# Gate rows as four products side by side, the last key transpose one tile later, and the branch stage's first operands over a token chunk, in a hybrid diffusion layer

## The chip, the cores and the metric

The kernel runs on one core of a Trainium2 chip. The metric is the device time of one execution in microseconds (us); the median of three runs of the kernel before is 2556.35 us (2554.89 to 2567.19). Engines are called as the profile calls them: PE (TensorE matmul), PEld (its weight load), DVE (VectorE), ACT (ScalarE), POOL (GpSimd) and SP (SyncE, which issues most of the transfers).

## What is computed

One layer of a hybrid backbone on 256 prompt tokens and 2048 latent tokens, width 1024, all in fp32:

```python
shift, scale, gate = split(silu(cond) @ w_mod + b_mod, 3)      # w_mod 1024 x 3072
xm = rmsnorm(x, norm_g) * (1 + scale) + shift
q, k, v, g_na, u, g_lru, c_b, c_c, c_h, g_conv, m_na, m_lru, m_conv = split(xm @ w_in)
o_na   = attention(q, k, v)            # prompt: dense; latents: neighbourhood + cached keys
h_f + h_b = two gated linear recurrences over conv4(u)
o_conv = c_b * conv3(c_c * c_h)
merged = ( sigmoid(m_na)   * ((o_na * silu(g_na))         @ w_br_na)
         + sigmoid(m_lru)  * (((h_f + h_b) * silu(g_lru)) @ w_br_lru)
         + sigmoid(m_conv) * ((o_conv * silu(g_conv))     @ w_br_conv) )
x = x + gate * (merged @ w_out);  y = rmsnorm(x, final_g)
# outputs: y of both groups, k and v of the prompt, final recurrence states
```

`cond` has two rows: one vector for the prompt, one for the latents. So `gate` is two rows of 1024 numbers.

## The kernel before

**Tokens and products.** Tokens stand in five chunks: chunk 0 is the prompt (256 tokens), chunks 1 to 4 are 512 latents each. A large product in fp32 is done as three passes of a split operand (high part and rest): `xh*whi`, `xl*whi`, `xh*wlo`. One 128-column tile of `w_in` times one 512-token chunk is thus 8 x 3 = 24 matmuls on PE into one bank of PSUM (tile `psM_C` is weight tile M with chunk C; `w_in_chunk`, L147 to L155). Only two chunks of latents and the prompt fit at a time, so the projection runs twice: with chunks in `ORDA` = (1, 2, 0), then in `ORDB` = (3, 4). The normalised chunks stand in tiles `xhA`/`xlA` (chunks 1, later 3) and `xhB`/`xlB` (2, later 4).

**Order.** Each engine takes its instructions in the order in which the program emits them. `dense` runs over weight tiles and chunks; a `Side` generator gets one step after each chunk (`tick`), and so lays recurrences, attention units or the gate rows between the chunks. Transfers are issued by SP in program order, a few by ACT. A transfer waits on its queue until the memory it writes is free, and all behind it wait too.

**Gate rows** (`gate_rows`, L382 to L399). The third kilocolumn of `w_mod` times the two condition vectors `sc`: for each half of 512 columns, eight products (one per 128 rows of `w_mod`) of two output rows each, `TE.matmul(pgt[:2, :], sc[:, kk - 1, :], ...)` in plain fp32, one after each chunk of the q and k tiles. The weights come in pieces `wg` of 256 KB, two buffers, one step ahead. Two sums on DVE (L398) add the bias.

**Prompt keys.** When tile 4+j has met the prompt chunk, the keys are copied to `kc` (ACT, L376) and put on a list; `key_out` (L343 to L351) transposes them on PE (`ktr`, two transposes) and stores them. For the last one this is called right after the last key tile (7), before tile 12.

**Branch stage and its memory** (L917 to L950). The last tiles of the projection (58 to 63, merge gates) run with ORDB; meanwhile the branch weights are loaded and split (`load_wb`). Then pool `p1` is closed, and the pool `zp` opens at the place in memory that is free. For chunk c and branches 2, 1, 0 it loads 1024 KB of branch outputs (`zr`, half of that for the prompt), splits them (`zh` on ACT, `zl` on DVE), loads eight `tg` tiles of gates, and does eight times 12 matmuls `pb`. Results are merged on POOL (L944) and stored by ACT (`d_mrg`). `zp` lies in memory over what `p1` held: weight buffers and chunk tiles. A first write into a place waits for the last reader of what lay there.

**Output stage** (L953 to L1000). Pool `op` opens where `zp` lay. `load_m` reads merged rows `mr`, splits them into `mh`, `ml`; PE does 24 matmuls `po` for each 128 tokens and half; the first 128 tokens come from tiles `m0h`, `m0l` that were made earlier. The first load of the stage is `mr128` (L958, called at L963).

Of the kernel before, what the change touches and what calls it, by code (L numbers as in the profile page):

```python
# [7 lines left out]
F32 = mybir.dt.float32  # L8
BF16 = mybir.dt.bfloat16
F32R = mybir.dt.float32r  # L10
AF = mybir.ActivationFunctionType
ALU = mybir.AluOpType
# [3 lines left out]
P = 128  # L16
D = 1024
KD = 8
# [3 lines left out]
ORDA, ORDB = (1, 2, 0), (3, 4)  # L22
# [22 lines left out]
def build(nc, tc, H):  # L45
    es = ExitStack()
    V, S, G, TE, SY = nc.vector, nc.scalar, nc.gpsimd, nc.tensor, nc.sync
# [25 lines left out]
    def scratch(name, shape):  # L73
        return tc.dram_tile(shape, F32, name=name)
# [9 lines left out]
    d_gna = scratch("d_gna", [512, T])  # L84
# [4 lines left out]
    d_sig = scratch("d_sig", [3072, T])  # L89
# [19 lines left out]
    sc = cp.tile([P, 8, 2], F32, tag="sc", name="sc")  # L109
# [9 lines left out]
    def bank(name):  # L119
        return psA.tile([P, 512], F32, tag="bank", name=name, bufs=8)  # L120


    p1 = ExitStack()
    ep = p1.enter_context(tc.tile_pool(name="ep", bufs=2))
    wp = p1.enter_context(tc.tile_pool(name="wp", bufs=2))
    xp = p1.enter_context(tc.tile_pool(name="xp", bufs=1))
    x0s = ExitStack()
    x0p = x0s.enter_context(tc.tile_pool(name="x0p", bufs=1))
    XS = {1: "A", 2: "B", 3: "A", 4: "B", 0: "0"}
# [8 lines left out]
    def load_w(m):  # L138
        hi = wp.tile([P, KD, P], F32R, tag="whi", name=f"whi{m}", bufs=3)
        lo = wp.tile([P, KD, P], F32R, tag="wlo", name=f"wlo{m}", bufs=3)  # L140
        for q in (0, 1):
            raw = wp.tile([P, 4, P], F32, tag="wraw", name=f"wraw{m}_{q}", bufs=4)
            SY.dma_start(raw, H["w_in"][m][:, 4 * q : 4 * q + 4, :])
            split(raw, hi[:, 4 * q : 4 * q + 4, :], lo[:, 4 * q : 4 * q + 4, :], G)
        return hi, lo

    def w_in_chunk(m, w, ci, evac):  # L147
        hi, lo = w
        t0, n = CH[ci]
        ps = bank(f"ps{m}_{ci}")  # L150
        ps_ = passes(KD)
        for i, (k, a, b) in enumerate(ps_):
            TE.matmul(ps[:, :n], (lo if a else hi)[:, k, :], (xl if b else xh)[ci][:, k, :],  # L153
                      start=(i == 0), stop=(i == len(ps_) - 1))
        evac(ci, t0, n, ps[:, :n])  # L155
# [8 lines left out]
    def ev_tanh(dst, j):  # L164
        def f(ci, t0, n, ps):
            o = ep.tile([P, 512], F32, tag="ev", bufs=3, name="evm")
            S.activation(o[:, :n], ps, AF.Tanh, scale=0.5)  # L167
            S.dma_start(dst[j * P : (j + 1) * P, t0 : t0 + n], o[:, :n])
        return f

    def ev_silu(dst, j):

        def f(ci, t0, n, ps):
            t = ep.tile([P, 512], F32, tag="evt", name="evt")
            o = ep.tile([P, 512], F32, tag="ev", bufs=3, name="evs")
            S.activation(t[:, :n], ps, AF.Tanh, scale=0.5)
            V.scalar_tensor_tensor(o[:, :n], t[:, :n], 1.0, ps, ALU.add, ALU.mult)
            SY.dma_start(dst[j * P : (j + 1) * P, t0 : t0 + n], o[:, :n])
        return f
# [17 lines left out]
    def dense(tiles, order, side=None):  # L197
        for m, evac in tiles:
            w = load_w(m)
            for ci in order:  # L200
                w_in_chunk(m, w, ci, evac)
                if side:
                    side.tick()
# [32 lines left out]
    with tc.tile_pool(name="p0", bufs=2) as p0:  # L236
# [13 lines left out]
        for kk in range(KD):  # L250
            wm = wms[kk // 2][:, kk % 2, :]
            SY.dma_start(wm, H["w_mod"][kk * P : (kk + 1) * P, 0 : 2 * D])
            for i in range(4):
                TE.matmul(pm[i][:2, :], sc[:, kk, :], wm[:, i * 512 : (i + 1) * 512],
                          start=(kk == 0), stop=(kk == KD - 1))
# [125 lines left out]

    def gate_rows(eq):  # L382

        for hf in (0, 1):
            hs = slice(512 * hf, 512 * hf + 512)
            bg = ep.tile([P, 512], F32, tag="evt", name=f"bg{hf}")
            SY.dma_start(bg[:2, :], H["b_gate"][:, hs].broadcast_to([2, 512]))
            pgt = bank(f"pgt{hf}")
            nxt = []
            for kk in range(KD + 1):  # L390
                if kk < KD:
                    wg = eq.tile([P, 512], F32, tag="wg", name=f"wg{hf}_{kk}", bufs=2)
                    SY.dma_start(wg, H["w_mod"][kk * P : (kk + 1) * P, 2048 + 512 * hf : 2560 + 512 * hf])
                    nxt.append(wg)
                if kk:
                    TE.matmul(pgt[:2, :], sc[:, kk - 1, :], nxt.pop(0), start=(kk == 1), stop=(kk == KD))
                yield
            V.tensor_tensor(bg[:2, :], pgt[:2, :], bg[:2, :], ALU.add)  # L398
            SY.dma_start(d_gate[:, hs], bg[:2, :])  # L399

    def cached_keys(eq):
# [248 lines left out]
    def flush():  # L650
        while pend or tpd:
            advance()
            yield
# [145 lines left out]
    def chain(*gens):  # L799
        for g in gens:  # L800
            yield from g
# [5 lines left out]
    with tc.tile_pool(name="eq", bufs=2, reuse_waits="tile") as eq, \  # L807
            tc.tile_pool(name="vcA", bufs=2, reuse_waits="tile") as vc, \
            tc.tile_pool(name="lp", bufs=1, reuse_waits="tile") as lp:
        lru = Side(lru_steps(lp, False), 17 / 84)  # L810
        gr = Side(gate_rows(eq), 1)
        dense([(j, ev_hilo(eq, d_q, j, 0.125, False)) for j in range(4)], ORDA,
              Side(iter(lambda: (lru.tick(), gr.tick()), None), 1))
        cached_keys(eq)
        dense([(4 + j, ev_hilo(eq, d_k, j, 1.0, True)) for j in range(4)], ORDA,
              Side(iter(lambda: (lru.tick(), gr.tick()), None), 1))
        gr.drain()
        while deferred:
            key_out(eq, *deferred.pop(0))
        dense([(12 + j, ev_silu(d_gna, j)) for j in range(4)], ORDA, lru)  # L820
        for j in range(4):
            dense(conv_tiles(vc, j, ORDA), ORDA, lru)
        lru.drain()
    with tc.tile_pool(name="atA", bufs=2, reuse_waits="tile") as at:
        AT[0] = at
        first_loads, units = latent_steps(at, [0])
        side = Side(chain(prompt_steps(at, first_loads), units, flush()), 60 / 60)
# [22 lines left out]
    with tc.tile_pool(name="lpB", bufs=1, reuse_waits="tile") as lp:  # L850
        lru = Side(lru_steps(lp, True), 25 / 76)
# [11 lines left out]
    with tc.tile_pool(name="atB", bufs=2, reuse_waits="tile") as at:  # L863
# [6 lines left out]
        side = Side(chain(units, flush()), 101 / 27)  # L870
# [4 lines left out]
    wbs = ExitStack()  # L875
# [13 lines left out]

    wks = (8, 9, 10, 11, 4, 5, 6, 7, 0, 1, 2, 3)  # L890
    for i, m in enumerate(range(18, 24)):
        dense([(40 + m, ev_tanh(d_sig, m))], ORDB)
        for k in wks[2 * i : 2 * i + 2]:
            load_wb(k)
    p1.close()

    wor = es.enter_context(tc.tile_pool(name="wor", bufs=1, reuse_waits="tile"))
    m0h = wor.tile([P, KD, P], F32R, tag="m0h", name="m0h")
    m0l = wor.tile([P, KD, P], F32R, tag="m0l", name="m0l")

# [15 lines left out]
    with tc.tile_pool(name="zp", bufs=2, reuse_waits="tile") as zp:  # L916
        for c in (0, 1, 2, 3, 4):  # L917
            t0, n = CH[c]
            cs = slice(t0, t0 + n)
            acc = []  # L920
            if c == 2:
                load_m0()
            for br in (2, 1, 0):
                zr = zp.tile([P, 4, 512], F32, tag="zraw", name=f"zr{c}_{br}", bufs=1)
                zh = zp.tile([P, 4, 512], F32R, tag="zh", name=f"zh{c}_{br}", bufs=3)
                zl = zp.tile([P, 4, 512], F32R, tag="zl", name=f"zl{c}_{br}", bufs=3)
                SY.dma_start(zr[:, :, :n], d_z[br * 512 : (br + 1) * 512, cs].rearrange("(k p) t -> p k t", p=P))
                for k in range(4):
                    split(zr[:, k, :n], zh[:, k, :n], zl[:, k, :n])
                for m in range(8):  # L930
                    t = zp.tile([P, 512], F32, tag="acc" if br == 2 else "tg", name=f"tg{c}_{br}_{m}",
                                bufs=9 if br == 2 else 6)
                    SY.dma_start(t[:, :n], d_sig[br * D + m * P : br * D + (m + 1) * P, cs])
                    ps = bank(f"pb{c}_{m}_{br}")
                    ps_ = passes(4)
                    for i, (k, a_, b_) in enumerate(ps_):
                        TE.matmul(ps[:, :n], (wbl if a_ else wbh)[br * 4 + k][:, m * P : (m + 1) * P],  # L937
                                  (zl if b_ else zh)[:, k, :n], start=(i == 0), stop=(i == len(ps_) - 1))

                    V.scalar_tensor_tensor(t[:, :n], t[:, :n], 1.0, ps[:, :n], ALU.add, ALU.mult)  # L940
                    if br == 2:
                        acc.append(t)
                    else:
                        G.tensor_tensor(acc[m][:, :n], acc[m][:, :n], t[:, :n], ALU.add)  # L944
                    if br == 0:
                        S.dma_start(d_mrg[m * P : (m + 1) * P, cs], acc[m][:, :n])
                if c == 4 and br:

                    for k in range(4):
                        load_wo(k + 4 * (2 - br), k + 4 * br)  # L950


    with tc.tile_pool(name="op", bufs=2, reuse_waits="tile") as op:  # L953
# [9 lines left out]
        nxt = load_m(P, P)  # L963
# [117 lines left out]
```

## Time and profile before

| | |
|---|---|
| median of three runs | 2556.35 us (2554.89 to 2567.19) |
| profiled execution, own time | 2558.7 us |
| its span (first to last instruction) | 2556.9 us |
| granted TensorE clock, mean | 0.989 |
| PE busy | 2492.1 us (97% of the span) |
| DVE / ACT / POOL busy | 1096.7 / 976.5 / 878.3 us |
| DMA | 360.84 MB, mean 141 GB/s |

PE is busy nearly all the time, so a microsecond is won either where PE has less to do, or in one of the few places where it waits. Busy counts overlap: a pipelined matmul of 512 columns has a duration of some 0.39 us in the list but starts 0.23 us after the one before it, so costs on PE are read from the distance of starts. A granted clock of 1.00 is 2.4 GHz and 0.50 is 1.2 GHz; after some of its waits PE runs a few us at the lower level.

### The profile page before, as it was taken

Reading aid. Unit: us, or ns where it says so; the run is one execution under the profiler, and the core shown is the slowest. Engines: PE = TensorE matmul, PEld = TensorE weight load, DVE = VectorE, ACT = ScalarE, POOL = GpSimd, SP = SyncE. Lnnn points to the kernel's source line nnn. Section 1 sums busy time; section 2 is a strip of 40 time slices with the busy share of each in tenths; the row PEclk is TensorE's granted clock in tenths of the full one; section 3 lists DMA queues with packets and bytes.
Section 4 is the critical chain, followed back from the end, with each engine's and each line's share of the span. In section 5 each row is a group of like instructions: output and inputs, shape, how many; then the busy total and the mean of one; then the engine's idle time right before and its main releaser. Section 6 shows DMA issues by size and latency. Waiting matters only on the chain. (4 is left out here: it accounts for less than half of the span.)

```text
span 2556.9 us, 35325 instructions
## 1 busy us (share of the span) xinstructions
PE 2492.1 (97%) x13192; PEld 2060.1 (81%) x13192; DVE 1096.7 (43%) x2329; ACT 976.5 (38%) x1849; POOL 878.3 (34%) x757
## 2 busy tenths in 40 slices
PE   8999999999999999999999998999999999999998
PEld 3887678888878888888888887778877788888887
DVE  5101244555223332314877873455544144333433
ACT  4311444344223334335766563445544311011221
POOL 2411223233542321332444444333331313335642
PEclk9999999999999999999999999999999999999999
DMA  7335552322743543345553326546552475555542
GB/s 280 110 91 153 160 132 84 75 58 65 185 118 107 155 146 136 101 133 117 185 162 120 118 87 183 170 142 179 170 145 82 148 239 181 181 161 189 176 137 83
DMA packets 248812, 360.84 MB, mean 141 GB/s; under 512 B 88761, under 2 KB 124729, under 8 KB 247617
## 3 DMA queue, kind: packets, MB, share of 16 engines
q1 hardware_dynamic: 147360, 227.20, 29.5%
q0 software_dynamic: 47920, 64.26, 9.0%
q10 hardware_dynamic: 53360, 67.13, 7.9%
q8 instruction: 104, 1.70, 0.3%
q14 instruction: 68, 0.55, 0.1%
HBM read 248.10 MB, written 110.11 MB: 140 GB/s over the span
## 5 line engine op out<-in xcount | busy, mean ns | idle before, releaser
L153 PE MATMUL ps<-xh,whi 128*128 128x512 f32 (+1 forms) x2400 | 899.8, 375 | 0.0
L153 PE MATMUL ps<-xl,whi 128*128 128x512 f32 (+1 forms) x2400 | 889.4, 371 | 2.1 <-DVE xl L56 1.6
L153 PE MATMUL ps<-xh,wlo 128*128 128x512 f32 (+1 forms) x2400 | 888.8, 370 | 0.0
L153 PEld LDWEIGHTS ps<-xh,whi 128*128 128x128 f32 x2400 | 455.9, 190 | 91.9 <-ACT qo L367 5.2
L56 POOL TENSOR_TENSOR wlo<-wraw,whi 128x512 fp32r<-128x512 f32 x240 | 336.2, 1418 | 550.9 <-ACT whi L55 491.3
L153 PEld LDWEIGHTS ps<-xl,whi 128*128 128x128 f32 x2400 | 456.0, 190 | 78.5 <-POOL xl L56 2.5
L153 PEld LDWEIGHTS ps<-xh,wlo 128*128 128x128 f32 x2400 | 455.3, 190 | 77.9
L55 ACT CAST whi<-wraw 128x512 fp32r<-128x512 f32 x240 | 144.9, 616 | 298.8 <-PE ps L153 168.4
L937 PE MATMUL pb<-zh,wbh 128*128 128x512 f32 (+1 forms) x480 | 179.0, 373 | 4.5 <-ACT zh L55 4.5
L937 PE MATMUL pb<-zl,wbh 128*128 128x512 f32 (+1 forms) x480 | 179.2, 373 | 0.0
L937 PE MATMUL pb<-zh,wbl 128*128 128x512 f32 (+1 forms) x480 | 179.1, 373 | 0.0
L167 ACT ACTIVATE evm<-ps 128x512 f32<-128x512 f32 (+1 forms) x120 | 66.4, 553 | 283.8 <-PE ps L153 282.9
L944 POOL TENSOR_TENSOR tg<-tg,tg 128x512 f32<-128x512 f32 (+1 forms) x80 | 97.0, 1223 | 188.2 <-DVE tg L940 183.4
L588 DVE TENSOR_SCALAR_CACHE_REDUCE p<-sc 128x256 f32<-128x256 f32 x127 | 53.2, 422 | 207.6 <-PE sc L583 206.9
L940 DVE SCALAR_TENSOR_TENSOR tg<-tg,pb 128x512 f32<-128x512 f32 (+1 forms) x120 | 74.9, 631 | 156.5 <-PE pb L937 146.6
L596 ACT ACTIVATE p<-p,ast 128x736 f32<-128x736 f32 (+2 forms) x127 | 109.6, 863 | 41.6 <-DVE ast L595 39.6
L444 DVE SCALAR_TENSOR_TENSOR uf<-ut,pk,uf 128x512 f32<-128x512 f32 (+1 forms) x120 | 104.2, 868 | 31.4 <-ACT uf L441 29.5
L613 PE MATMUL t<-ident,p 128*128 128x128 f32 x698 | 98.7, 275 | 18.9 <-DVE p L598 17.3
L475 POOL TENSOR_TENSOR sq<-sq,ea 128x512 f32<-128x512 f32 (+1 forms) x40 | 61.9, 1549 | 153.5 <-ACT sq L468 94.7
L55 ACT CAST zh<-zr 128x512 fp32r<-128x512 f32 (+1 forms) x60 | 30.5, 575 | 212.3 <-PE pb L937 99.9
L617 ACT COPY pT<-t 128x512 f32<-128x512 f32 (+3 forms) x256 | 95.3, 407 | 37.4 <-PE t L613 37.4
L937 PEld LDWEIGHTS pb<-zh,wbh 128*128 128x128 f32 x480 | 90.8, 189 | 22.3 <-ACT zh L55 5.0
(233 smaller groups left out, 3639.2 us busy)
## 6 DMA issues: line engine op xcount, KB each, us to landing
wraw<-w_in SPq DMA_DIRECT2D x240, 256.0 KB, 3.8
d_sig<-evm ACTq DMA_DIRECT2D x96, 256.0 KB, 4.0
tg<-d_sig SPq DMA_DIRECT2D x96, 256.0 KB, 4.0
xt<-x SPq DMA_DIRECT2D x36, 512.0 KB, 4.2
qs<-d_q POOLq DMA_DIRECT2D x32, 512.0 KB, 17.9
zr<-d_z SPq DMA_DIRECT2D x12, 1024.0 KB, 5.5
d_mrg<-tg ACTq DMA_DIRECT2D x32, 256.0 KB, 4.5
mr<-d_mrg SPq DMA_DIRECT2D x8, 1024.0 KB, 5.8
```

The source lines that it names most:

```text
L55: S.copy(hi, src)
L56: lo_eng.tensor_tensor(lo, src, r2f(hi), ALU.subtract)
L153: TE.matmul(ps[:, :n], (lo if a else hi)[:, k, :], (xl if b else xh)[ci][:, k, :], start=(i == 0), stop=(i == len(ps_) - 1))
L167: S.activation(o[:, :n], ps, AF.Tanh, scale=0.5)
L444: V.scalar_tensor_tensor(uf[:, :n], ut[:, tap : tap + n], cw(tap), uf[:, :n], ALU.mult, ALU.add)
L475: G.tensor_tensor(sq[:, :n], sq[:, :n], ea[:, :n], ALU.mult)
L596: S.activation(p[:, :nk], p[:, :nk], AF.Exp, bias=st[:, 2:3], accum_out=st[:, 3:4])
L613: TE.transpose(tb[:, ti * P : ti * P + P], p[:, c0 : c0 + P], ident)
L617: S.copy(pT[:, base : base + last - first], tb[:, first:last])
L937: TE.matmul(ps[:, :n], (wbl if a_ else wbh)[br * 4 + k][:, m * P : (m + 1) * P], (zl if b_ else zh)[:, k, :n], start=(i == 0), stop=(i == ...
L940: V.scalar_tensor_tensor(t[:, :n], t[:, :n], 1.0, ps[:, :n], ALU.add, ALU.mult)
L944: G.tensor_tensor(acc[m][:, :n], acc[m][:, :n], t[:, :n], ALU.add)
```

## The change

There are three edits and what follows from them.

1. `gate_rows`: four loads of 1 MB (256 rows and all 1024 gate columns of `w_mod`, one buffer) instead of sixteen of 256 KB. After each, three steps later, four products follow each other on PE, with outputs at partitions 0, 32, 64 and 96 of one bank (two row blocks x two halves). DVE then adds two partial rows for each half (four sums instead of two).
2. The last `key_out` comes after weight tile 12 instead of before it.
3. Pool `xp` (chunk tiles) is opened first and has the lowest place. The last tile (63) meets chunk 4 first, then 3. `zh` and `zl` get a tag for each of three buffers, so that their order in memory is fixed; the pool `wor` moves to the right side. The `zp` tiles of the first steps now lie where chunk 4 (`xhB`, `xlB`) was.

```diff
+    xp = p1.enter_context(tc.tile_pool(name="xp", bufs=1))
     ep = p1.enter_context(tc.tile_pool(name="ep", bufs=2))
     wp = p1.enter_context(tc.tile_pool(name="wp", bufs=2))
-    xp = p1.enter_context(tc.tile_pool(name="xp", bufs=1))
...
     def gate_rows(eq):
+        pgt = bank("pgt")
+        for kp in range(KD // 2):
+            wg = eq.tile([P, 2, D], F32, tag="wg", name=f"wg{kp}", bufs=1)
+            SY.dma_start(wg, H["w_mod"][256 * kp : 256 * kp + 256, 2048:3072].rearrange("(a p) c -> p a c", p=P))
+            yield
+            yield
+            yield
+            for i in range(4):
+                a, hf = i // 2, i % 2
+                TE.matmul(pgt[32 * i : 32 * i + 2, :], sc[:, 2 * kp + a, :], wg[:, a, 512 * hf : 512 * hf + 512],
+                          start=(kp == 0), stop=(kp == KD // 2 - 1))
+            yield
         for hf in (0, 1):
...
-            pgt = bank(f"pgt{hf}")
-            nxt = []
-            for kk in range(KD + 1):
-                if kk < KD:
-                    wg = eq.tile([P, 512], F32, tag="wg", name=f"wg{hf}_{kk}", bufs=2)
-                    SY.dma_start(wg, H["w_mod"][kk * P : (kk + 1) * P, 2048 + 512 * hf : 2560 + 512 * hf])
-                    nxt.append(wg)
-                if kk:
-                    TE.matmul(pgt[:2, :], sc[:, kk - 1, :], nxt.pop(0), start=(kk == 1), stop=(kk == KD))
-                yield
-            V.tensor_tensor(bg[:2, :], pgt[:2, :], bg[:2, :], ALU.add)
+            for a in (0, 1):
+                i = 2 * a + hf
+                V.tensor_tensor(bg[:2, :], pgt[32 * i : 32 * i + 2, :], bg[:2, :], ALU.add)
...
+        dense([(12, ev_silu(d_gna, 0))], ORDA, lru)
         while deferred:
             key_out(eq, *deferred.pop(0))
-        dense([(12 + j, ev_silu(d_gna, j)) for j in range(4)], ORDA, lru)
+        dense([(12 + j, ev_silu(d_gna, j)) for j in (1, 2, 3)], ORDA, lru)
...
-        dense([(40 + m, ev_tanh(d_sig, m))], ORDB)
+        dense([(40 + m, ev_tanh(d_sig, m))], ORDB if m < 23 else ORDB[::-1])
...
-    wor = es.enter_context(tc.tile_pool(name="wor", bufs=1, reuse_waits="tile"))
+    wor = wbs.enter_context(tc.tile_pool(name="wor", bufs=1, side="right", reuse_waits="tile"))
...
-                zh = zp.tile([P, 4, 512], F32R, tag="zh", name=f"zh{c}_{br}", bufs=3)
-                zl = zp.tile([P, 4, 512], F32R, tag="zl", name=f"zl{c}_{br}", bufs=3)
+                zi = (3 * c + 2 - br) % 3
+                zh = zp.tile([P, 4, 512], F32R, tag=f"zh{zi}", name=f"zh{c}_{br}", bufs=1)
+                zl = zp.tile([P, 4, 512], F32R, tag=f"zl{zi}", name=f"zl{c}_{br}", bufs=1)
```

The order of SP's transfers in the stretch of the q tiles (weight tiles 0 to 3), before the change; `wg0_4` is the piece of half 0 and row block 4, `d_q` are stores of finished q, `wraw` the raw `w_in` weights:

```order
L393 DMA wg0_4_1885<-w_mod 128x512
L355 DMA d_q_57<-evl_1824 128x512
L393 DMA wg0_5_1919<-w_mod 128x512
L355 DMA d_q_57<-evl_1860 128x512
L393 DMA wg0_6_1965<-w_mod 128x512
L355 DMA d_q_57<-evl_1914 128x256
L143 DMA wraw6_0_2523<-w_in 128x512
L143 DMA wraw6_1_2527<-w_in 128x512
L393 DMA wg0_7_2001<-w_mod 128x512
```

The same stretch of SP after the change:

```order
L388 DMA wg1_1878<-w_mod 128x2x1024
L355 DMA d_q_57<-evl_1816 128x512
L355 DMA d_q_57<-evl_1853 128x512
L143 DMA wraw6_0_2502<-w_in 128x512
L355 DMA d_q_57<-evl_1906 128x256
L143 DMA wraw6_1_2506<-w_in 128x512
L355 DMA d_q_57<-evl_1947 128x512
L388 DMA wg2_2022<-w_mod 128x2x1024
```

One load of 1 MB stands where four of 256 KB and more stood, and three stores of q lie between the first of these loads and the products that use it.

PE around the last key transpose, before the change: it stands between weight tile 7 and weight tile 12.

```order
L153 MATMUL ps7_0_2771<-xl0_507,whi7_2688 128x256
L153 MATMUL ps7_0_2771<-xh0_506,wlo7_2689 128x256
L346 MATMUL ktr_2806<-ident_73,kc_2804 128x128 x2
L153 MATMUL ps12_1_2823<-xh1_222,whi12_2813 128x512
L153 MATMUL ps12_1_2823<-xl1_223,whi12_2813 128x512
```

PE around the same transposes after the change:

```order
L153 MATMUL ps12_0_2906<-xl0_507,whi12_2783 128x256
L153 MATMUL ps12_0_2906<-xh0_506,wlo12_2784 128x256
L346 MATMUL ktr_2936<-ident_73,kc_2781 128x128 x2
L153 MATMUL ps13_1_2953<-xh1_222,whi13_2943 128x512
L153 MATMUL ps13_1_2953<-xl1_223,whi13_2943 128x512
```

They now have three chunks of weight tile 12 between the keys' copy and themselves.

ACT at the start of the branch stage, before the change (`evm` is the eviction of a finished `ps`, `d_sig` its store, `zh` the split of the first branch operand):

```order
L167 ACTIVATE evm_18088<-ps63_3_18063 128x512
L168 DMA d_sig_67<-evm_18088 128x512
L167 ACTIVATE evm_18116<-ps63_4_18091 128x512
L168 DMA d_sig_67<-evm_18116 128x512
L55 CAST zh0_2_18147<-zr0_2_18146 128x256 x4
```

ACT at the same place after the change:

```order
L167 ACTIVATE evm_18065<-ps63_4_18040 128x512
L168 DMA d_sig_67<-evm_18065 128x512
L167 ACTIVATE evm_18093<-ps63_3_18068 128x512
L168 DMA d_sig_67<-evm_18093 128x512
L55 CAST zh0_2_18124<-zr0_2_18123 128x256 x4
```

The two chunks have changed places; the split of `zh0_2` stands behind both evictions and both stores, as it did. The load `zr0_2` itself waits for the matmuls of `ps63_4`, which are now the last but one group on PE instead of the last. The second transfer behind it on SP, `tg0_2_1`, waits for the last matmul of `ps63_3`. In the output stage the load `mr128` now lies over buffers of the last merged tile, and waits for the stores `d_mrg` of chunk 4; before, it lay over a place that was free early.

## Rows read from the trace of the kernel before

**Rows 1.** Page, part 1: busy time of each engine.
```profile
PE 2492.1 (97%) x13192; PEld 2060.1 (81%) x13192; DVE 1096.7 (43%) x2329; ACT 976.5 (38%) x1849; POOL 878.3 (34%) x757
```

**Rows 2.** Waits of PE: line, releaser, us in total, times, longest.
```profile
PE pb L937 <- ACT zh L55: 4.5, 1, 4.5
...
PE ktr L346 <- ACT kc L376: 4.2, 1, 4.2
...
PE pgt L396 <- DMA wg<-w_mod: 2.2, 1, 2.2
```

**Rows 3.** Chain of waits, its end: start us, us, what.
```profile
2041.97 4.20 DMA zr<-d_z
...
2046.70 303.55 PE pb L937 x1440
2350.26 197.79 PE po L986 x864
```

**Rows 4.** Timeline of PE at one gate product: start us, us, instruction.
```profile
310.10 0.39 PE L153 MATMUL ps<-xl,whi 128*128 128x512 f32 x1
310.32 0.39 PE L153 MATMUL ps<-xh,wlo 128*128 128x512 f32 x1
310.64 1.02 PE L396 MATMUL pgt<-wg,sc 128*2 128x512 f32 x2
311.59 0.50 PE L153 MATMUL ps<-xh,whi 128*128 128x512 f32 x1
311.93 0.40 PE L153 MATMUL ps<-xl,whi 128*128 128x512 f32 x1
```

**Rows 5.** Tile wg: durations in ns min/median/max, and its transfers' landing.
```profile
L396 PE MATMUL pgt<-wg,sc x32: 591/592/592, 227.7 to 321.9; 128*2 128x512 f32 x32
...
DMA to landing us min/median/max: 2.7/3.1/6.0
```

**Rows 6.** Line L628, attention outputs, 64 output columns each: durations in ns.
```profile
L628 PE MATMUL o<-pT,vb x896: 219/272/324, 810.4 to 1971.4; 128*64 128x128 f32 x103, 128*64 128x64 f32 x42, 96*64 96x64 f32 x35
```

**Rows 7.** Timeline of PE, first two matmuls of an attention output alone.
```profile
1944.48 0.33 PE L628 MATMUL o<-pT,vb 128*64 128x128 f32 x2
```

**Rows 8.** Timeline of PE, the same attention output in whole.
```profile
1944.48 0.66 PE L628 MATMUL o<-pT,vb 128*64 128x128 f32 x8
1944.97 0.61 PE L628 MATMUL o<-pT,cv 128*64 128x128 f32 x8
```

**Rows 9.** Timeline of PE at the last key transpose.
```profile
356.30 0.69 PE L346 MATMUL ktr<-ident,kc 128*128 128x128 f32 x2 [4.17 <-ACT kc L376]
356.64 0.78 PE L153 MATMUL ps<-xh,whi 128*128 128x512 f32 x1
```

**Rows 10.** Windows: length, busy us and instructions of each engine, PEclk, DMA share, GB/s.
```profile
304.00:310.00 6.00, 5.97 (x24) 4.27 (x25) 1.41 (x3) 3.71 (x7) 2.55 (x2) 1.00 0.84 230
356.30:361.30 5.00, 5.00 (x13) 4.03 (x14) 0.42 (x1) 1.24 (x1) 0.00 (x0) 0.50 0.68 209
2046.70:2051.00 4.30, 4.30 (x21) 4.13 (x22) 1.84 (x5) 0.87 (x3) 0.00 (x0) 0.60 0.94 284
```

**Rows 11.** Timeline of ACT at the start of the branch stage.
```profile
2042.20 0.60 ACT L167 ACTIVATE evm<-ps 128x512 f32<-128x512 f32 x1 [4.84 <-PE ps L153]
2042.83 0.36 ACTq L168 DMA_DIRECT2D d_sig<-evm  x1
2046.25 1.32 ACT L55 CAST zh<-zr 128x256 fp32r<-128x256 f32 x4 [3.45 <-DMA zr<-d_z]
```

**Rows 12.** Timeline of SP at the start of the output stage.
```profile
2343.70 0.37 SPq L958 DMA_DIRECT2D mr<-d_mrg  x1
```

**Rows 13.** Timeline of ACT at the start of the output stage.
```profile
2349.64 3.15 ACTq L946 DMA_DIRECT2D d_mrg<-tg  x2
2352.88 1.70 ACT L55 CAST mh<-mr 128x128 fp32r<-128x128 f32 x8 [16.77 <-DMA d_mrg<-tg]
```

**Rows 14.** Tile mr: its nine transfers' landing.
```profile
DMA to landing us min/median/max: 4.9/5.6/6.3
```

**Rows 15.** Tensor d_mrg: its transfers' landing.
```profile
DMA to landing us min/median/max: 2.5/4.7/8.5
```

## Prediction

> **What bounds the kernel now.** I read the page's busy times first: PE works 2492.1 of 2556.9 us [rows 1], so what counts is PE's work and PE's waits. Then the waits of PE: three of them, 4.5, 4.2 and 2.2 us, stand at the places that the change touches [rows 2]. The chain shows that the first of the three is on the path to the end: a load `zr` is issued at 2041.97 and takes 4.20 us, and from 2046.70 PE goes through without another wait [rows 3]. Timelines of PE, ACT and SP give the prices, and the windows show the granted clock behind each wait. A price on PE is a distance between starts, not a duration: `ps` matmuls of 512 columns start 0.22 to 0.23 us apart (310.10 to 310.32; I use 0.227) though each is listed with 0.39 [rows 4].
>
> **Gate rows.** One product between two `ps` matmuls: from 310.32 to 311.93 are 1.61 us in which two `ps` starts (0.45) would have passed, so it costs 1.16 us [rows 4]. A product is two passes of 0.592 us each [rows 5] that span 1.02 [rows 4], so they start 0.43 apart; two passes hold PE for 0.86, and 0.30 goes into the change from split matmuls to plain ones and back. Sixteen products cost 18.5 us, and the wait for one late `wg` adds 2.2 [rows 2]: 20.7.
>
> After the change four products with outputs in four separate groups of 32 partitions come together, four times. The trace has no such four, but it has pairs: attention outputs of 64 columns, two side by side. A matmul of 128 columns should take a quarter of the 0.43 for 512, 0.107 us; eight of them one behind the other 0.86. They take 0.49 (1944.48 to 1944.97) [rows 8]. And the first two together end 0.33 us after the start, when one alone takes up to 0.324 [rows 6, 7]: the second starts 6 ns after the first. So pairs run side by side from their first pass. If four do the same, a group costs 1.16 + 3 x 0.006 = 1.18 us, four groups 4.7, and 20.7 - 4.7 = 16.0 us go. Bounds: if nothing runs side by side, a group is 8 x 0.43 + 0.30 = 3.74, four are 15.0, and 5.7 go (the 2.2 of the wait among them). I take 16.0, since the second of a pair starts without a wait; the 0.06 by which 0.49 exceeds four slots of 0.107 would be some 0.5 us over all groups.
>
> The Trainium skill is less generous: "TensorE: Matmul & The Clock Gate", section "Measured speedup vs the span model", gives a measured 2.38 times for three tiles side by side in columns. With the same share lost, four would give 3.17 times, by which I estimate 4 x 1.16 / 3.17 = 1.46 us for a group and 1.1 us less gain in all. No run here shows four; the pairs of rows 8 gain 0.86/0.49 = 1.75 of 2, a similar share.
>
> What hides the rest: each 1 MB load has three chunks, 2 x 24 x 0.227 + 24 x 0.12 = 13.7 us (half chunk: half the columns), between its issue and its use; loads of `mr`, also 1 MB but the first, land in 4.9 to 6.3 us [rows 14]. The single buffer is free once the group before has run, one chunk earlier. Stores of q that stand behind a waiting `wg` are late by no more than one step. If this cover failed by 2 us, it would cost those 2 us and, as below, the clock. The two sums that DVE gains stand off the path, on an engine that is busy for 43% of the span [rows 1]. I put all this at 0 to -2, and take 0. The old wait of 2.2 us had no clock loss behind it: 1.00 from 304 to 310 [rows 10].
>
> **Key transposes.** PE waits 4.17 us for the copy `kc` [rows 9], and then runs 5.0 us at a granted 0.50 [rows 10], that is 1.2 GHz: what took 5.0 would take 2.5, so 2.5 more are lost. After the change three chunks of tile 12 (13.7 us) stand between the copy and the transposes. The weights of tile 12 are split while tile 7 runs (three buffers), so PE has work at once; both transposes cost the same wherever they stand. The saving is 4.2 without the clock and 6.7 with it. What could be late next is tile 12's eviction or its weights, behind the same copy on ACT; eight PSUM banks cover the first. I take 6.5.
>
> **Branch operands.** `zr0_2` now waits for the last matmul of chunk 4, which is 24 x 0.227 = 5.4 us before the last matmul. It is issued at 2036.5 in the old frame and lands at 2040.7 [rows 3]. But the wait does not go in whole: on ACT the splits of `zh0_2` stand behind the last chunk's eviction and store, and those follow PE: 2042.20 to 2043.19 [rows 11]. The first split ends 0.45 later (2046.25 to 2046.70 [rows 3, 11]), at about 2043.65. PE's wait falls from 4.5 to 1.5 us: 3.0 saved. After the old wait the window of 4.3 us had 0.60 [rows 10], so 1.7 us were lost. Whether a wait of 1.5 us still brings the clock down can't be read: after 2.2 us at the gate it stayed at 1.00. Bounds 0 and 1.7; I take half, 0.9. Sum 3.9, between 3.0 and 4.7. Behind `tg0_2_1`, which waits on SP for the last `ps`, are six gate tiles and the next `zr`; in the old frame they were issued after that moment too, so they are no later.
>
> **Output stage.** `mr128` was issued at 2343.70 [rows 12], long before its use. Now it waits for the last stores of merged rows. The last is issued by 2352.79 (2349.64 + 3.15 [rows 13]) and lands 2.5 to 4.7 us after its issue at 2352.4 or so (minimum and median [rows 15]): 2355 to 2357. The load takes 4.9 to 5.6 [rows 14] and lands at 2360 to 2363; two splits add 0.5. PE needs it after 48 matmuls of 197.79/864 = 0.229 us [rows 3], at 2361.2. So PE waits 0 to 2.0 us, with up to as much for the clock. `gb`, `fg`, `xt` and `mr256` are queued behind `mr128` and start together; the first results on DVE and POOL come some 6 us later than before, and `ml256` is split behind them on POOL, where up to 1 us can come out late. All: 0 to -5, nearer to 0 since the quieter stores take the minimum; I take -1.0.
>
> **Sum.** 16.0 + 6.5 + 3.9 - 1.0 = 25.4 us. The profiled execution took 2558.7, so 2533.3; the median of the runs is 2.35 lower than it, so I predict 2531 against 2556.35, about 1.0% less. PE's other waits (attention, start) stay as they are: they hang on operands that follow PE.
>
> **Rivals.**
> *Products in steps.* PE takes matmuls strictly in order: the second pass of a product must wait for its first, 0.43 us, and all products behind it wait too; only the second pass of one and the first of the next overlap. A group is five slots, 5 x 0.43 + 0.30 = 2.45, four are 9.8, and 10.9 instead of 16.0 go: 2536. Against it stands the 6 ns of rows 7; for it, that the eight of rows 8 take 0.49, between four slots (0.43) and five (0.54). The Trainium skill's page named above, "What overlaps and what doesn't", has it that matmuls start and end strictly in program order, which would bring this about if both passes of a product are issued before the next; rows 7 speak against that order.
> *No overlap at all.* 5.7 instead of 16.0: 2541. The pairs speak against it, but four moving streams of fp32 are twice what the pairs need.
> *The boundary stays as it is.* If PE waits as long as before because ACT's splits or DVE's are held by something else, 3.9 goes: 2535.
> *Slower: the output stage starts late and stays late.* `mr128` holds SP's queue until the last merged store; each later `mr` uses one of two buffers that the splits free. If POOL, which would then start 6 us late, set the pace, each of nine loads would hold PE by its landing and two splits less the cover. To turn the sum into a loss of over 0.5%, the stage must cost 25.4 + 1.0 + 12.8 = 39 us, 4.4 for each of nine loads: 2570. It decides only if no block makes up what the first lost. For it: POOL's position behind `y`. Against: PE has 96 x 0.229 = 22 us for each 256 tokens while a load and its splits need some 6 + 11.
>
> **How the numbers follow.** The forecast has 70%, its own range 2529 to 2537: at the one end all of the clock at the boundary and nothing at the output stage (0.8 + 1.0 + 0.2 of the key), at the other 1.1 less at the gate, 0.9 at the boundary and 4.0 at the output stage. Steps 12%, no overlap 6%, boundary unchanged 7%, late output 3%; the rest is a new wait that I don't see, up to some 10 us. The range 2524 to 2543 takes in the first three rivals (2535 to 2541) and, at both ends, some us for clock stretches and small waits that come or go where the order around these places shifts; it leaves out 2 in 10 at most. 0.5%, about what a measurement of this kernel can tell from no change, is 12.8 us: faster means below 2543.6. The first four cases lie there, most with room: 0.87. No change holds a lost gate gain together with a new wait: 0.09; slower 0.04.
>
> **What would show it.** In the changed kernel: each group of gate products 1.2 us between `ps` starts (2.4: steps; 3.7: none side by side), no wait at `pgt`; no wait at `ktr` and 1.00 where 0.50 stood; `pb` waits about 1.5 us on ACT instead of 4.5; `mr128` issued near the last store's landing, and a PE wait below 2 us at `po`. The forecast is wrong if groups cost over 2.4, if a new wait of PE over 3 us appears, or if PE's time in the branch or output stage grows.

## The result, and the profile after

The changed kernel takes 2542.94 us (median of five runs, 2536.39 to 2545.32) against 2556.35 (five runs, 2552.97 to 2567.19). The two medians are 13.4 us apart; the ratio of the runs is 0.9931, 95% interval 0.9917 to 0.9946, or 18 us less (14 to 21). The forecast was 2531, 25 us less, in a range of 2524 to 2543. So the direction was right, and between a third and a half of the gain is missing. The median lies inside the range by 0.06 us, far less than the runs scatter: that it is inside is luck. The profiled execution took 2536.39 us, span 2534.1: 22.8 us less than the span before.

Page, part 1, of the changed kernel, beside [rows 1]:

```profile
PE 2472.3 (98%) x13192; PEld 2053.4 (81%) x13192; DVE 1097.5 (43%) x2331; ACT 976.2 (39%) x1849; POOL 877.6 (35%) x757
```

PE is busy for 19.8 us less with the same number of instructions. The waits of PE in the changed kernel, line, releaser, total, times, longest, beside [rows 2]:

```profile
PE ktr L346 <- ACT kc L376: 3.4, 2, 2.4
...
PE pb L946 <- ACT zh L55: 1.8, 1, 1.8
...
PE po L995 <- POOL ml L56: 0.4, 1, 0.4
```

The wait at `pgt` is gone and the one at `pb` fell from 4.5 to 1.8. But `ktr` still waits: not once for 4.2, but twice, at two *other* transposes. The timeline of PE in the changed kernel at a group of gate products, beside [rows 4]:

```profile
236.37 0.39 PE L153 MATMUL ps<-xh,wlo 128*128 128x512 f32 x1
236.69 1.04 PE L394 MATMUL pgt<-wg,sc 128*2 128x512 f32 x8
237.66 0.50 PE L153 MATMUL ps<-xh,whi 128*128 128x512 f32 x1
237.99 0.40 PE L153 MATMUL ps<-xl,whi 128*128 128x512 f32 x1
```

From 236.37 to 237.99 are 1.62 us, where one product took 1.61: four products now cost what one did, 1.17 us. And PE at the transposes of key tiles 1 and 2 (counted from 0):

```profile
319.27 0.44 PE L346 MATMUL ktr<-ident,kc 128*128 128x128 f32 x2 [1.04 <-ACT kc L376]
...
337.26 0.44 PE L346 MATMUL ktr<-ident,kc 128*128 128x128 f32 x2 [2.40 <-ACT kc L376]
```

To see where the time went I compare the same matmul in both traces: the 7200 matmuls of L153 counted from 0 in order of start. The table has the distance of starts in us. *Gate* is matmul 624 to 1008, *keys* 1008 to 1224 (the last key tiles and tile 12), *prompt* 2900 to 3098 (prompt attention, whose instructions no edit touches), *boundary* the last of L153 to the 200th `pb`, *output* the first 120 `po`. In gate_kc_free and all_together some recurrence steps stand elsewhere, so their *gate* and *keys* don't compare with the other rows.

| kernel | gate | keys | prompt | boundary | output |
|---|---|---|---|---|---|
| before | 93.8 | 51.0 | 54.1 | 29.5 | 27.5 |
| after | 78.9 | 47.9 | 55.4 | 25.2 | 28.4 |
| after, second profile | 78.9 | 50.3 | 54.7 | 26.1 | 28.0 |
| gate_only | 78.9 | 57.6 | 59.6 | 29.9 | 27.5 |
| key_only | 92.7 | 44.2 | 54.7 | 30.6 | 27.5 |
| boundary_only | 92.8 | 51.6 | 55.8 | 24.9 | 28.1 |
| keys_late | 78.8 | 46.0 | 54.5 | 24.9 | 28.6 |
| gate_kc | 78.9 | 51.3 | 58.6 | 29.5 | 27.5 |
| after_kc | 78.9 | 44.3 | 54.4 | 25.8 | 28.2 |
| gate_pairs | 82.3 | 47.3 | 55.0 | 26.1 | 27.8 |
| gate_rowwise | 82.3 | 49.6 | 58.0 | 25.2 | 28.3 |
| after_kc_mr | 78.9 | 45.7 | 53.9 | 24.9 | 27.4 |
| gate_kc_free | 77.5 | 44.6 | 55.1 | 30.7 | 27.5 |
| all_together | 77.5 | 43.3 | 54.4 | 25.8 | 27.4 |

The gate gave 14.9 (and 1.0 for the first product, which lies ahead of matmul 624): 15.9. The boundary gave 4.3, the output stage took 0.9. The keys gave only 3.1, or 0.7 in the second profile, where 6.5 were forecast. With the first profile the four parts sum to 22.4, and the spans differ by 22.8: in this execution what is missing from the forecast's 25.4 is the keys' 3.4. (The wait at `pgt`, 2.2 us in the profile before, is 1.1 and 1.2 in key_only and boundary_only, which have the old gate rows; so some 1 us of the 15.9 varies between executions.)

### The profile page after: what moved, and what is told of

Its sections match the earlier page's. It is cut to its first block, busy times and chain, and to the rows that moved or that the text cites. A ratio compares the mean times of both kernels' runs of the same rounds, so it can differ in the third digit from the quotient of the medians.

```text
span 2534.1 us, 35302 instructions
## 1 busy us (share of the span) xinstructions
PE 2472.3 (98%) x13192; PEld 2053.4 (81%) x13192; DVE 1097.5 (43%) x2331; ACT 976.2 (39%) x1849; POOL 877.6 (35%) x757
## 5 line engine op out<-in xcount | busy, mean ns | idle before, releaser
L153 PE MATMUL ps<-xh,whi 128*128 128x512 f32 (+1 forms) x2400 | 896.3, 373 | 0.0
L153 PE MATMUL ps<-xl,whi 128*128 128x512 f32 (+1 forms) x2400 | 887.5, 370 | 3.5 <-POOL xl L56 1.9
L153 PE MATMUL ps<-xh,wlo 128*128 128x512 f32 (+1 forms) x2400 | 886.5, 369 | 0.0
L153 PEld LDWEIGHTS ps<-xh,whi 128*128 128x128 f32 x2400 | 454.3, 189 | 81.2 <-issue 2.6
L153 PEld LDWEIGHTS ps<-xl,whi 128*128 128x128 f32 x2400 | 454.5, 189 | 79.6 <-POOL xl L56 3.7
L153 PEld LDWEIGHTS ps<-xh,wlo 128*128 128x128 f32 x2400 | 454.2, 189 | 77.5
L55 ACT CAST zh<-zr 128x512 fp32r<-128x512 f32 (+1 forms) x60 | 30.6, 575 | 208.7 <-PE pb L946 149.2
L618 PEld LDWEIGHTS t<-ident,p 128*128 128x128 f32 x698 | 82.6, 142 | 30.8 <-DVE p L603 18.9
```

The costliest lines, as they stand in the source:

```text
L55: S.copy(hi, src)
L618: TE.transpose(tb[:, ti * P : ti * P + P], p[:, c0 : c0 + P], ident)
```

## The experiments

Theory 1: the gate's gain is partly given back at the key transposes, since PE comes to them earlier while the copies `kc` on ACT do not. Theory 2: the parts add without touching each other, and what is missing is scatter of the clock elsewhere.

| kernel | median us (runs) | ratio to before, 95% interval |
|---|---|---|
| gate_only | 2555.22 (11) | 0.9978 [0.9967, 0.9989] |
| key_only | 2550.97 (9) | 0.9969 [0.9957, 0.9980] |
| boundary_only | 2553.41 (12) | 0.9980 [0.9970, 0.9989] |
| keys_late | 2535.34 (6) | 0.9911 [0.9896, 0.9925] |
| gate_kc | 2549.90 (7) | 0.9957 [0.9939, 0.9974] |
| after_kc | 2534.85 (5) | 0.9902 [0.9885, 0.9920] |
| gate_kc_free | 2537.15 (4) | 0.9914 [0.9897, 0.9931] |
| after_kc_mr | 2535.84 (4) | 0.9908 [0.9893, 0.9923] |
| after_again | 2541.53 (6) | 0.9936 [0.9921, 0.9951] |
| all_together | 2535.18 (4) | 0.9895 [0.9879, 0.9912] |
| gate_pairs, gate_rowwise | 2543.02, 2545.45 (1 each) | one run each, no ratio |

**gate_only**: the diff's `gate_rows` alone, all else as before.

> Only the gate rows are changed; key order, pools and last tile as before. Theory 1 (the gate's gain is partly given back at the key transposes, since PE comes to them earlier while ACT, held by its d_k stores, does not): gate groups 1.2 us each, PE ahead by 15 to 16 us at the end of the products, then new waits at the transposes of key tiles 1 and 2 (1.0 and 2.4 us in the changed kernel) and at the last one at least the old 4.2 us; net 9 to 12 us below before. Theory 2 (parts add, no interaction): only the old 4.2 us wait at the last transpose, net 15 to 16 us below before.

0.9978: 5.6 us (3 to 8) of the 15.9. The products cost what they cost in the changed kernel (78.9), but the key stretch grew from 51.0 to 57.6. The waits of PE in gate_only, and its timeline of ACT at the last `kc`:

```profile
PE ktr L346 <- ACT kc L376: 9.4, 3, 6.4
```

```profile
342.54 0.38 ACT L371 ACTIVATE evh<-ps 128x256 fp32r<-128x256 f32 x1
342.82 0.61 ACT L55 CAST whi<-wraw 128x512 fp32r<-128x512 f32 x1
343.56 3.86 ACTq L358 DMA_DIRECT2D d_k<-evh  x2
347.47 0.37 ACT L376 COPY kc<-ps 128x256 f32<-128x256 f32 x1 [4.04 <-DMA o_k<-ko]
```

PE had finished this key tile at 341.5; the copy came six us later, because ACT issues the stores of the split keys first, and the second of the two was held until a transfer had ended which the profile names as `o_k<-ko`, the store of the *previous* key tile. The semaphores in the trace bear this out: both transfers report their end on the same one (number 102), `o_k` landed at 346.95, and the held store was issued at 346.98. One wait of 4.2 became three, 9.4 in all. So theory 2 is out for the key stretch. Gate and keys together leave 15.9 - 6.6 = 9.3 us, inside theory 1's range of 9 to 12; the runs show less, 5.6. The rest is not explained: in this profile the prompt stretch is 5.5 us longer than before as well, but its waits for `kp` vary from 4.3 to 8.8 us between the profiles, and nothing shown ties them to the change.

**key_only**: the diff's move of the last `key_out` alone.

> Only the last key transpose is moved behind weight tile 12. Theory 1: its wait of 4.2 us and the half clock behind it go, no other transpose waits because PE is not early; 6 to 7 us below before in the profile at tile 13. Rival (the chain on ACT and the stores that hold it bound this stretch, the wait moves to a later matmul): under 3 us.

0.9969, 8 us; the key stretch falls from 51.0 to 44.2, by 6.8, and no `ktr` waits. The forecast's 6.5 was right, as long as PE is not early.

**boundary_only**: pools, order of the last tile's chunks and tags alone.

> Only the pools' places, the order of the last tile's two chunks and the tags of zh and zl are changed. Forecast: PE waits 1.8 instead of 4.5 us at the first branch matmul, with at most a short stretch of half clock; 3 to 4 us less there, 0 to 1 us lost at the first matmuls of the output stage; 2.5 to 4 us below before. Rival (the output stage gives it all back): 0 to 1 us.

0.9980, 5 us (3 to 8), and 29.5 to 24.9 at the boundary, 0.6 lost at the output stage. The three parts alone sum to 0.22 + 0.31 + 0.20 = 0.73%, the changed kernel has 0.69%: so the sum is right with the gate at 5.6 us, not at 16.

**keys_late**: the changed kernel, with the first three transposes one chunk later.

```diff
                 deferred.append((kc, j))
-            elif deferred and ci == 2:
-                key_out(eq, *deferred.pop(0))
+                if len(deferred) > 1:
+                    key_out(eq, *deferred.pop(0))
```

> The changed kernel, with the transposes of the first three key tiles one chunk later too (after the prompt chunk of the next key tile instead of after its second latent chunk). Theory 1: the waits of 1.0 and 2.4 us and the clock behind them go, 3 to 4 us below the changed kernel in the profile. Theory 2 (the rest to the forecast is scatter of the clock elsewhere): the waits were covered time, no gain at tile 13.

0.9911 instead of 0.9931: some 5 us, though the two intervals overlap (0.9896 to 0.9925 here), with 1.6 us of waiting at `ktr` left. The key stretch takes 46.0, 1.9 us less than in the first profile of the changed kernel and 4.3 less than in the second; 3 to 4 were expected. In line with theory 1, but the gain at tile 13 is hardly larger than what two profiles of one kernel differ by.

**gate_kc** and **after_kc**: gate_only and the changed kernel, with `kc` copied before the keys are evicted and stored; PE's program is the same.

```diff
             lo = eq.tile([P, 512], F32R, tag="evl", name="evl")
+            if keep and ci == 0:
+                kc = eq.tile([P, 256], F32, tag="kc", bufs=2, name="kc")
+                S.copy(kc, ps)
...
             if keep and ci == 0:
-                kc = eq.tile([P, 256], F32, tag="kc", bufs=2, name="kc")
-                S.copy(kc, ps)
                 deferred.append((kc, j))
```

> The kernel before with the gate rows of the change and one more edit: the copy of the prompt keys (kc) stands ahead of the eviction and its stores on ACT instead of behind them; the transposes stay where they were on PE. Theory 1 (gate_only lost its gain because kc stands on ACT behind stores that wait for other transfers): the three waits at ktr (2.0, 1.0 and 6.4 us in gate_only) shrink to about 1 us in all, the key stretch takes 44 to 47 us instead of 57.7, and the kernel comes out 16 to 21 us below before. Rival (ACT as a whole, its recurrence work included, is late, wherever kc stands): the waits stay above 5 us in sum and the kernel is 5 to 9 us below before, as gate_only.

> The changed kernel with the same edit on ACT. Theory 1: the waits of 1.0 and 2.4 us at the transposes of key tiles 1 and 2 go, 3 to 4 us below the changed kernel, 20 to 25 us below before. Rival: no gain over the changed kernel.

after_kc: 0.9902, 25 us less than before, as much as was forecast for the change; no `ktr` in its list of waits, 44.3 in the key stretch. PE's program is that of the changed kernel, so the place of `kc` on ACT was what took the gain. The margin is thin: the third copy ends at 333.00 and its transposes start at 333.06, and after_kc_mr below, with the same edit, waits once more for 1.4 us. gate_kc: 0.9957, half of what theory 1 said: 5.1 us of waits are left, 3.7 of them at the last transpose, which in this kernel follows its tile at once:

```profile
337.52 0.60 ACT L447 ACTIVATE uf<-ut,pk 128x256 f32<-128x256 f32 x1 [1.99 <-DVE sq L484]
338.03 1.12 ACT L55 CAST whi<-wraw 128x512 fp32r<-128x512 f32 x2
339.06 0.59 ACT L374 ACTIVATE evh<-ps 128x512 fp32r<-128x512 f32 x1
339.68 1.10 ACTq L358 DMA_DIRECT2D d_k<-evh  x2
340.88 0.62 ACT L55 CAST whi<-wraw 128x512 fp32r<-128x512 f32 x1 [1.23 <-POOL wlo L56]
341.40 0.36 ACT L366 COPY kc<-ps 128x256 f32<-128x256 f32 x1
```

That is ACT of gate_kc: ahead of `kc` stands a step of the recurrence (`uf`), which waited 1.99 us for DVE, then weights (one of them waited 1.23 us for POOL), the eviction of the chunk before and its stores. Neither theory 1 alone nor its rival. The edit puts `kc` ahead of the whole eviction and not of the stores alone, and in the changed kernel the late copies had waited last for DVE's part of it (`evl`; 1.40 us at key tile 2). So what it shows is that eviction and stores together take about half; the next run is about the rest.

**gate_kc_free**: gate_kc with the recurrence's steps taken out from between the key tiles (rate 17/72 in place of 17/84, `gr` alone as side work there).

> gate_kc with no recurrence step between the chunks of the four key tiles (the same steps come more densely in the other tiles). It tests what is left of the waits at the transposes in gate_kc (5.1 us: 1.4 and 3.7). Theory A (the kc copies still come late because ACT has recurrence work and what that waits for ahead of them): the waits at ktr fall below 2.5 us in all; the kernel 2 to 4 us below gate_kc unless the denser steps cost elsewhere. Theory B (the stores alone hold ACT): the waits stay at 4 us or more.

0.9914, and the waits at `ktr` fall to 0.9 us. Theory A. By the ratios that is 11 us below gate_kc, more than the 4 us of waits and the 2 to 4 us expected. The two profiled executions are only 5.0 us apart in span (2544.0 and 2539.0); the one of gate_kc is among the shorter of its runs and that of gate_kc_free is the longest of its four. Where the rest comes from is open.

**gate_pairs** and **gate_rowwise**: the changed kernel with two column groups; the four products use them in the order 0, 1, 0, 1, or 0, 0, 1, 1 (the sums on DVE follow; not shown).

```diff
-                a, hf = i // 2, i % 2
-                TE.matmul(pgt[32 * i : 32 * i + 2, :], ...
+                hf, a = i // 2, i % 2                # gate_rowwise alone
+                TE.matmul(pgt[32 * hf : 32 * hf + 2, :], ...
```

> The changed kernel with only two column groups: the products of both row blocks accumulate at partitions 0 and 32, in the order block 0 half 0, block 0 half 1, block 1 half 0, block 1 half 1. If products with different groups run fully side by side: 2 x 0.86 + 0.30 = 2.0 us a group of four, 0.84 more than the changed kernel. If none does: 3.7.

> As gate_pairs with the order block 0 half 0, block 1 half 0, block 0 half 1, block 1 half 1, so that neighbours in the program share a column group. If PE starts matmuls strictly in program order: only the second and third product can overlap, 3.2 to 3.4 us a group. If it lets a free group go ahead of one that waits: 2.0 us as gate_pairs.

PE at one group, gate_pairs first, then gate_rowwise, the latter with its first 0.2 us alone:

```profile
235.85 0.39 PE L153 MATMUL ps<-xh,wlo 128*128 128x512 f32 x1
236.16 1.89 PE L394 MATMUL pgt<-wg,sc 128*2 128x512 f32 x8
237.98 0.50 PE L153 MATMUL ps<-xh,whi 128*128 128x512 f32 x1
238.31 0.39 PE L153 MATMUL ps<-xl,whi 128*128 128x512 f32 x1
```

```profile
236.01 0.39 PE L153 MATMUL ps<-xh,wlo 128*128 128x512 f32 x1
236.33 1.89 PE L394 MATMUL pgt<-wg,sc 128*2 128x512 f32 x8
238.15 0.50 PE L153 MATMUL ps<-xh,whi 128*128 128x512 f32 x1
238.49 0.39 PE L153 MATMUL ps<-xl,whi 128*128 128x512 f32 x1
```

```profile
236.33 0.60 PE L394 MATMUL pgt<-wg,sc 128*2 128x512 f32 x2
```

Both take 2.0 us (2.46 and 2.48 less 0.45), also the one whose neighbours in the program share a group; in program order 3.2 to 3.4 were expected. There two matmuls start within the first 0.2 us. The profile doesn't say which products they are. But 2 x 0.86 + 0.30 = 2.0 is the time of two products one behind the other in each of two groups that run side by side; and the second start comes 13 ns after the first (236.332 and 236.345), two of the steps of 6 to 7 ns by which products of different groups follow each other in gate_pairs and in the changed kernel. So I read them as the first product and the third: one of the free group went ahead of one that waited. The rival of products in steps (2.45 for four groups) is refuted by the 1.17 of the changed kernel and, as far as it rests on strict order, once more here.

**after_kc_mr**: after_kc, with the tile `mr` allocated ahead of `mh` and `ml` in the output stage.

> after_kc, with the tile mr allocated first in the output stage's pool, so that mr128 lies over the zr buffer and not over merged tiles, and is issued before the last d_mrg stores. If the late mr128 costs the 0.7 to 0.9 us at the start of the output stage: the first 120 po matmuls take 27.5 us as before instead of 28.2. If that loss has another cause: 28.2. The time changes by less than can be measured.

27.4 us for the first 120 `po`: the loss (0.7 in after_kc, 0.9 in the changed kernel) came from the late `mr128`, which holds up what is queued behind it. In time (0.9908 and 0.9902) no difference can be seen. Beside after_again, the next run, which was timed against the same runs of before, it tells best what copying `kc` first is worth (with `mr` first, which is worth less than 1 us): 2534.96 to 2536.56 us in four runs against 2536.27 to 2548.19 in six.

**after_again**: the changed kernel once more.

> The changed kernel once more, for a second profile beside those of the same chip: the key stretch should again take about 47.9 us with waits at two transposes, while the stretches of attention, where no part of the change works, may differ by some us from its first profile. Ratio to before 0.992 to 0.995.

0.9936. Waits of 1.6 and 2.7 us at `ktr`, and this time the clock fell behind them:

```profile
337.80:341.30 3.50, 3.50 (x19) 3.50 (x18) 3.43 (x6) 1.63 (x3) 2.04 (x2) 0.51 0.84 237
```

The window of 3.5 us has a granted clock of 0.51; in the first profile there was none. So this stretch took 50.3, not 47.9: 0.9 us more of waiting, and half of 3.5 us for the clock.

**all_together**: the changed kernel with `kc` first, no recurrence between the key tiles, `mr` first.

> The changed kernel with the three edits that removed waits: kc ahead of the stores, no recurrence steps between the key tiles, mr first. If the pieces add: no wait over 1 us at ktr, the boundary wait at 1.5 to 1.8 us, the first po matmuls at 27.4 to 27.6 us, and a ratio to before of 0.987 to 0.990 (gate_kc_free has 0.9914 with the old boundary, whose change alone gave 0.998). If the key stretch has nothing more to give once its waits are gone: 0.990 to 0.992, as after_kc.

0.9895, with no wait at `ktr`, 1.5 us at `pb` and 27.4 at the output stage. It is the lowest of the ratios and lies in the first of the two ranges (0.987 to 0.990), but its interval, 0.9879 to 0.9912, reaches through the second and holds the ratios of after_kc and after_kc_mr. Whether what gate_kc_free gained over gate_kc is added once the keys wait no more, these runs don't tell.

## Why the prediction was right in direction and too high in size

- **Gate rows: right on PE.** 1.17 us a group (1.18 forecast), no wait at `pgt`, 15.9 us at the end of the products (16.0). No new wait came from the 1 MB loads, though they landed in 6.7 to 11.7 us, not 4.9 to 6.3: the cover of 13.7 us held. The lower gain by the Trainium skill's "TensorE: Matmul & The Clock Gate", "Measured speedup vs the span model" (1.46 us by my estimate) does not show here: 4 x 1.16 / 1.17 is 3.97 of 4.
- **Key transposes: the step that failed.** The term was 6.5 us. The text said: "What could be late next is tile 12's eviction or its weights, behind the same copy on ACT", and "PE's other waits [...] stay as they are". I costed the last transpose with PE where it stood before. But the gate term puts PE 15 us earlier at the same ACT queue, and two transposes that had never waited now do: 3.4 us in the first profile, 4.3 and some clock in the second. The term measured 3.1 and 0.7 instead of 6.5. The trace of the kernel before has the slack that should have been read. There the copies of key tiles 1 and 2, and the transposes that use them, stand at

```profile
326.12 0.37 ACT L376 COPY kc<-ps 128x256 f32<-128x256 f32 x1 [3.24 <-issue]
333.48 0.38 PE L346 MATMUL ktr<-ident,kc 128*128 128x128 f32 x2
...
346.19 0.37 ACT L376 COPY kc<-ps 128x256 f32<-128x256 f32 x1 [1.42 <-DVE evl L372]
348.87 0.38 PE L346 MATMUL ktr<-ident,kc 128*128 128x128 f32 x2
```

  so they had 7.0 and 2.3 us to spare, against 15 that PE gained; in the changed kernel the same copies start at 318.85 and 336.84, only 7.3 and 9.4 us earlier. key_only shows that 6.5 holds without the gate; after_kc, with the copies ahead of the eviction, gives 25 us (20 to 29), the forecast's sum.
- **Boundary: right.** `pb` waits 1.77 us (1.5 forecast) on ACT's split behind both evictions, as the text had it. The clock stayed up, which I had at half: in the changed kernel the window that had 0.60 in [rows 10] reads

```profile
2025.10:2029.40 4.30, 4.23 (x35) 4.07 (x36) 2.27 (x6) 0.94 (x4) 0.00 (x0) 1.00 0.62 196
```

  Together 4.3 instead of 3.9.
- **Output stage: size right (0.9 for 1.0), by one of the two ways named.** The forecast had PE wait for `mr128` itself (0 to 2.0 us), and up to 1 us for `ml256`, split behind POOL's late work. Only the second came. `mr128` was issued at 2331.43, 0.1 us after the last store had landed, and was split in time. What came late was queued behind it; lines from the chain of waits of the changed kernel show it:

```profile
2329.29 2.01 DMA d_mrg<-tg
...
2333.43 8.62 DMA xt<-x
...
2342.19 1.24 POOL y L998
...
2352.14 0.75 POOL ml L56
...
2352.93 7.17 PE po L995 x30
```

  `xt` landed 8.62 us after its issue, POOL's `y` waited for it, and `ml256` behind it was late: PE idled 0.36 us at the 108th `po`, and with three more late starts among the next four it lost the 0.9. The rival in which the stage stays late did not come: the rest of the stage takes 170.1 us in both. (Of the signs that the forecast named against itself, this is the one that came, by less than a microsecond: PE's time in the output stage grew. The new waits of PE stay below its 3 us.)
- **What stays open.** Both profiles of the changed kernel (2536.39 and 2536.27 us) are the shortest of their runs; the others take 2540.8 to 2548.2, and have no trace. After_kc's five runs lie at 2530 to 2537. I think that the key stretch and its clock make part of this difference; no trace shows it, and theory 2, scatter elsewhere, is not out for it. Of scatter the traces have enough: from matmul 3098 to the last one of L153, where no edit changes the instructions but for the order of the last tile's chunks, the fourteen profiles take 1274.7 to 1280.8 us, and the two of the changed kernel, with 1276.8 and 1274.7, are among the shortest. In keys_late and gate_pairs the rest of the output stage takes 173.4 instead of 170.1, with no wait and a granted clock of 1.00. The mean granted clock, which is on record for every run, is 0.993 and 0.992 in the two profiled executions and 0.989 to 0.992 in the other nine.

## What to carry to other kernels

When work is taken off the engine that sets the pace, look at every wait downstream that was *nearly* a wait, not only at those in the list: here 15 us less on PE brought it to copies that had 7.0 and 2.3 us to spare, and that themselves came only 7.3 and 9.4 us earlier. A copy that the pacing engine waits for belongs ahead of evictions and stores on its queue: here one store's issue was held by a transfer of another tile. Do each part alone as well as all: the three parts' sum agreed with the whole, and yet by the runs the largest part had lost two thirds of its gain, of which the table shows 6.6 us at the keys.

## What the runs showed of the hardware

- Four plain fp32 products of two rows, on four groups of 32 columns, take the time of one (1.17 and 1.16 us); on two groups 2.0.
- Two matmuls whose column groups differ need not start in program order: in gate_rowwise the group of four takes 2.0 us, and the second start, 13 ns after the first, is read as the third product of the program.
- A wait of 1.5 to 1.8 us at the boundary left the clock at 1.00 in all nine profiles with the new boundary; one of 4.5 us was followed by 0.60. At the transposes the length of the wait alone doesn't tell: one of 2.4 us left the clock up in the changed kernel, but one of 2.7 in its second profile was followed by 0.51, one of 2.0 in gate_only (321.5 to 324.8) and one of 2.1 in gate_rowwise (341.8 to 345.2) by 0.50.
- An issue of a transfer on ACT was held for nearly 3 us by a transfer that SP had issued, where both used one completion semaphore (gate_only, 344.02 to 346.98).
